# Layer norm's affine part as two fused operations on VectorE, sums of quarters reordered, last transposes among the first products, other banks in the recurrence

## The chip, the cores and the metric

The kernel runs on one core of one Trainium2 chip. A core has a matrix engine (TensorE, PE in the profile, with its weight loads as PEld), three engines for elementwise work (VectorE = DVE, ScalarE = ACT, GpSimd = POOL), and SyncE (SP), whose queue issues the transfers. SBUF is the memory on the core that the engines work on, PSUM its accumulators, of which this kernel uses eight banks of 128x512 fp32. The metric is device microseconds of one execution: the median of three runs. The profile is of one further execution, in which the hardware profiler records start and end of the instructions.

## The reference

One step of a trunk of two layers, over a prompt of 1024 tokens and 8 samples of 8 tokens (1088 tokens in all), width 1024, all in fp32. Each layer is a mixer (layer 0: RG-LRU, layer 1: HGRN2 with 8 heads) and a gated ffn with a causal convolution of width 3, both followed by a layer norm:

```python
def layer_norm(x, g, b):
    mu = jnp.mean(xf, axis=-1, keepdims=True)
    var = jnp.mean(jnp.square(xf - mu), axis=-1, keepdims=True)
    y = (xf - mu) * lax.rsqrt(var + LN_EPS) * g + b

def conv_ffn(x, buf, w_in, cw, cb, w_out):
    gate, up = jnp.split(x @ w_in, 2, axis=-1)          # 1024 -> 2 x 2816
    gc, new_buf = causal_dwconv(gate, buf, cw, cb)
    return (jax.nn.gelu(gc) * up) @ w_out, new_buf      # 2816 -> 1024

for i in range(DEPTH):                                  # trunk, DEPTH = 2
    mix = rglru_mixer(x, ...) if i % 2 == 0 else hgrn2_mixer(x, ...)
    x = layer_norm(ALPHA * x + mix, ln_g[i, 0], ln_b[i, 0])
    x = layer_norm(ALPHA * x + conv_ffn(x, ...), ln_g[i, 1], ln_b[i, 1])
```

The HGRN2 mixer projects x to q, f, v and g, forms decays from f, and per head and chunk of 64 tokens adds a masked product of q, k and the decays times v to what the carried state gives. Its output is normalised, gated by g and projected back. Besides the 1088 rows of output, the last states of both recurrences and of the convolutions are returned.

## The kernel before

**Precision.** Every fp32 matrix is split into a high part (rounded to the type fp32r) and a low part (the rest), and each product is three matmuls: high x high, high x low, low x high. So every weight and every activation must be split: one copy on ACT gives the high part, one subtraction on DVE or POOL the low part.

**Tiles and phases.** Tokens are tiled by 128: tiles m = 0 to 7 are the prompt, tile 8 holds the 64 sample tokens. z holds one row of 1024 fp32 per token; xa holds the transposed, split activations that feed the products. The phases are: mixer of layer 0 and its output projection (mix_out), ffn of layer 0 (phase 1), the HGRN2 mixer and its mix_out (phase 2), ffn of layer 1 (phase 3).

**The order of work is written by hand**: the instructions of each engine stand in the order in which the Python code calls them, and each engine runs its own in that order, waiting on semaphores for the others. `steps` is the list of steps, each with its weight blocks. A block's raw fp32 load is issued by SP (L140) into one of the buffers raw and rawf; `convert` splits it into a buffer of kind "b" (three, wb) or of kind "x" (wxf and wxb, there only inside an ffn, wx and wr elsewhere), with the high part on ACT (L214) and the low part on POOL or DVE (L215). A buffer comes free when its step ends. Work that may be squeezed between products waits in the queue `pend`: `fill()` runs one item, `flush()` all of them.

**The ffn's first product** is done on quarters, with 7 products of sums of quarters in place of 8 products. The activations' quarters b11, b21, b12, b22 come from the transposes of two tiles m and m + 4, four PSUM banks; `to_sums(m)` forms the seven sums and splits each (xc[0] to xc[6]): `put(c, src, eng)` is a high part on ACT (L392) and a low part on DVE or POOL (L393); L395 to L402 form the sums in scratch space of z. `to_sums(4)` does the samples. The weights' seven sums per block are formed by POOL (L176 to L182), split by ACT (L185) and POOL (L186). The first block of each ffn runs all seven products for the first 288 columns (the samples and the pairs 0 and 1), which accumulate in the four banks of psi, then for the other 256 (pairs 2 and 3), in the four banks of pss. `fills` gives the work to be called after product (i, c), i being the product and c the half.

**Layer norm** runs as a pipeline over tiles in `ln_pipeline`: `step_m` does the last projection of a tile and adds it to z (L413, with the row sums), `nrm_a` makes the row statistics on ACT (L424 to L426), `nrm_b` refines the reciprocal root on DVE (L431 to L434), normalises (L436, DVE) and multiplies by gamma (L438, on POOL, on DVE for the last two tiles of a mixer's norm), and `nrm_c` adds beta (L451, DVE) and stores the row (L456, to zsave or to the output). nrm_b runs one tile behind and nrm_c two; three behind comes `turn`, the transposes for the next phase. Behind a mixer the order of tiles is 8, 0, 4, 1, 5, 2, 6, 3, 7, so that to_sums(0) can begin after tile 4; the last two turns stand at i = 9 and in pend. The very last tile of the kernel is split between DVE (768 columns) and POOL (256).

**The ffn's second product** takes the 22 tiles of gelu(gate) * up in three groups. They are stored to ysave as they come and loaded again into xa; `y_part` splits them in two pieces, high on ACT (L1142), low on DVE (L1143). The last group takes four weight blocks and is the step inside the norm's pipeline.

**The recurrence** works by heads in periods: DVE and ACT make decays and scaled copies, PE grams (L1448), transposes (`kt_small`, L1533 and L1536), state products (`p_small`, with DVE's L1564 as evacuation), outputs (`o_small`), and the projections for the coming heads (`in_chunk`, L298 to L300, in psi banks) and for v (`v_step`, L1656 to L1658). `sbank` hands out a PSUM bank: of psi where run["bank"] is "in", else of pss.

Of the kernel before, what the change touches and what calls it, by code (L numbers as in the profile page):

```python
# [19 lines left out]
D = 1024  # L20
# [40 lines left out]
def hawk_hgrn2_convffn_deepnorm_kernel(  # L61
# [45 lines left out]
    run = {"dve": (), "ch": CH, "dma": 0, "cvt": 0, "phase": -1, "n": 0, "lo": dve}  # L107
# [86 lines left out]
    def convert():  # L194
# [166 lines left out]
    def to_sums(mp):  # L361
# [32 lines left out]

        act.copy(t1, b12)  # L395
        dve.tensor_tensor(t3, b22, t1, ALU.subtract)
# [31 lines left out]
    def nrm_b(m):  # L428
# [6 lines left out]
        for _, c in parts(m):  # L435
            dve.tensor_scalar(z[:r, m, c], z[:r, m, c], st[:, 2:3], st[:, 7:8], ALU.add, ALU.mult)  # L436
        for eng, c in parts(m):
            eng.tensor_tensor(z[:r, m, c], z[:r, m, c], gb[:r, 0, c], ALU.mult)  # L438

    def parts(m):  # L440

        if run.get("end") == m:
            return (pool, slice(768, D)), (dve, slice(0, 768))
        if m in run["dve"]:
            return (dve, slice(0, D)),
        return (pool, slice(0, D)),

    def nrm_c(m, final):
        r = rows_of(m)
        for eng, c in parts(m) if final == "out" and m >= NT - 3 else ((dve, slice(0, D)),):  # L450
            eng.tensor_tensor(z[:r, m, c], z[:r, m, c], gb[:r, 1, c], ALU.add)  # L451
# [10 lines left out]
    def ln_pipeline(step_m, junk, final=None, between={}, sums=False):  # L462
# [5 lines left out]
        run["dve"] = order[-2:] if sums else ()  # L468
# [7 lines left out]
        for i in range(NT + 2):  # L476
# [512 lines left out]
    def ffn(phase, li, final):  # L989
# [148 lines left out]
        def y_part(f, i):  # L1138

            y = yv[i]  # L1140
            for hi, lo in ((y[:, :SEQ], y[:, U + NS:]), (y[:, SEQ:U], y[:, U:U + NS])):
                act.copy(hi, lo.bitcast(F32))  # L1142
                dve.tensor_tensor(lo, lo.bitcast(F32), hi, ALU.subtract)  # L1143
# [40 lines left out]
        for p in range(NP):  # L1184
            f0, f1 = 2 * p, 2 * p + 1

            def gates(b, p=p, f0=f0, f1=f1):
# [3 lines left out]
                else:  # L1191
                    fills = {(5, 0): [flush]}
# [32 lines left out]
        for gi, grp in enumerate(GROUPS):  # L1225
# [27 lines left out]
            else:  # L1253
# [10 lines left out]
                stepf(phase, [out_blk(WO, f0, 0), out_blk(WO, f0, 1), out_blk(WO, f0 + 2, 0), out_blk(WO, f0 + 2, 1)], fn, "aaaa")  # L1264
# [260 lines left out]
    def kt_small(h):  # L1525
# [4 lines left out]
        for b0 in (0, 4):  # L1530
            ps = sbank("ps_kt")
# [295 lines left out]
```

## Time and profile before

| | us |
|---|---|
| median of 3 runs | 2615.56 (2613.95 to 2618.47) |
| the profiled execution | 2615.03 |
| its span, first to last instruction | 2613.3 |
| PE busy | 2506.9 (96%) |
| DVE busy | 1559.5 (60%) |
| POOL busy | 1378.8 (53%) |
| ACT busy | 951.9 (36%) |

The mean granted TensorE clock was 0.981 of full speed. A busy share is over the whole span; each phase has limits of its own. A row of waits names the waiting engine, the tile and line, what ended the wait, and the total, the number and the longest in us. A row of the timeline has the start and the duration in us, engine, line, operation, out<-in, shape and count; behind it, in brackets, the idle time ahead of it and what ended that. Lines such as L451 are those of the listing above. Records of a few matmuls are missing from the trace.

### The profile page before, as it was taken

The page shows a single profiled execution, that of the slowest core. Times are in us where ns is not written, and L with a number is a line of the kernel's source. Part 1 is how long each engine was busy: PE and PEld are TensorE (multiplying, and loading weights), DVE is VectorE, ACT ScalarE, POOL GpSimd, SP SyncE. Part 2 cuts the span into 40 slices and gives each one's busy share as a digit, 9 for nine tenths or more (in the row PEclk, how much of TensorE's full clock was granted, in tenths as well). Part 3 has the DMA queues.
Part 4 walks back from the last instruction along what each step waited for, and adds up shares of the span by engine and source line. Part 5 has one row for each costly group of instructions (what it writes and reads, how often), then busy time and mean ns, then how long its engine had stood idle before and what let it go on. Part 6 is the DMA issues. An engine that isn't in the chain of part 4 may idle for free. (4 is left out here: it accounts for less than half of the span.)

```text
span 2613.3 us, 39952 instructions
## 1 busy us (share of the span) xinstructions
PE 2506.9 (96%) x16007; PEld 2317.7 (89%) x16007; DVE 1559.5 (60%) x2431; ACT 951.9 (36%) x1643; POOL 1378.8 (53%) x1150
## 2 busy tenths in 40 slices
PE   9999969999999999999999999999799999999997
PEld 8999869999999788789898999977699999988886
DVE  4987376565656333658758485875656565562327
ACT  4775243333334011334444353453333333330113
POOL 2534378888876122235444452525788887842114
PEclk9999989999999999999999999999899999999999
DMA  4114022222224322122111111122222223264111
GB/s 131 41 45 165 32 81 66 84 66 91 74 85 169 134 100 83 49 83 58 48 34 42 50 42 42 50 88 99 73 84 67 83 67 95 77 227 136 58 41 72
DMA packets 205839, 209.79 MB, mean 80 GB/s; under 512 B 13201, under 2 KB 167953, under 8 KB 205614
## 3 DMA queue, kind: packets, MB, share of 16 engines
q1 hardware_dynamic: 205654, 207.25, 24.6%
q8 instruction: 126, 2.06, 0.3%
q14 instruction: 59, 0.48, 0.1%
HBM read 159.61 MB, written 47.61 MB: 79 GB/s over the span
## 5 line engine op out<-in xcount | busy, mean ns | idle before, releaser
L215 POOL TENSOR_TENSOR wb<-raw,wb 128x1024 fp32r<-128x1024 f32 (+1 forms) x77 | 201.2, 2616 | 618.4 <-ACT wb L214 415.7
L1057 PE MATMUL ps_f<-xa,wb 128*128 128x288 f32 (+1 forms) x3072 | 399.7, 290 | 15.0 <-ACT z L395 6.8
L1062 DVE TENSOR_TENSOR z<-z,ps_f 128x256 f32<-128x256 f32 (+2 forms) x550 | 196.0, 378 | 357.0 <-PE ps_f L1057 300.6
L1057 PEld LDWEIGHTS ps_f<-xa,wb 128*128 128x128 f32 x3072 | 392.5, 189 | 18.1 <-ACT z L395 7.6
L1057 PE MATMUL ps_f<-x,wb 128*128 128x288 f32 (+1 forms) x2496 | 323.0, 289 | 2.4 <-POOL wb L186 1.3
L1057 PEld LDWEIGHTS ps_f<-x,wb 128*128 128x128 f32 x2496 | 318.1, 189 | 3.2 <-POOL wb L186 1.7
L298 PE MATMUL ps_in<-xa,wb 128*128 128x384 f32 (+3 forms) x912 | 306.4, 336 | 5.7 <-ACT wb L214 5.5
L299 PE MATMUL ps_in<-xa,wb 128*128 128x384 f32 (+3 forms) x912 | 299.6, 329 | 0.3 <-DVE xa L356 0.3
L300 PE MATMUL ps_in<-xa,wb 128*128 128x384 f32 (+3 forms) x912 | 299.7, 329 | 0.0
L413 DVE SCALAR_TENSOR_TENSOR z<-z,ps_fo 128x512 f32<-128x512 f32 x128 | 87.8, 686 | 279.0 <-PE ps_fo L1162 266.5
L186 POOL TENSOR_TENSOR wb<-raw,wb 128x512 fp32r<-128x512 f32 x116 | 163.2, 1413 | 66.5 <-ACT wb L185 56.2
L186 POOL TENSOR_TENSOR wb<-rawf,wb 128x512 fp32r<-128x512 f32 x116 | 165.6, 1436 | 56.8 <-ACT wb L185 56.8
L214 ACT CAST wb<-raw 128x1024 fp32r<-128x1024 f32 (+1 forms) x83 | 82.0, 989 | 298.6 <-issue 183.1
L1110 DVE SCALAR_TENSOR_TENSOR z<-z,ptf 128x1104 f32<-128x1104 f32 x88 | 182.5, 2074 | 1.6
L298 PEld LDWEIGHTS ps_in<-xa,wb 128*128 128x128 f32 x912 | 172.9, 190 | 8.4 <-ACT wb L214 5.7
L299 PEld LDWEIGHTS ps_in<-xa,wb 128*128 128x128 f32 x912 | 173.1, 190 | 1.4 <-DVE xa L356 0.7
L300 PEld LDWEIGHTS ps_in<-xa,wb 128*128 128x128 f32 x912 | 172.4, 189 | 1.4 <-DVE wb L215 0.8
L1057 PE MATMUL ps_f<-xa,wxf 128*128 128x256 f32 (+1 forms) x1152 | 149.8, 288 | 2.7 <-ACT z L1077 2.7
L1057 PEld LDWEIGHTS ps_f<-xa,wxf 128*128 128x128 f32 x1152 | 146.6, 189 | 3.1 <-ACT z L1077 3.1
L185 ACT CAST wb<-rawf 128x512 fp32r<-128x512 f32 x116 | 71.1, 624 | 209.8 <-POOL rawf L182 76.0
L438 POOL TENSOR_TENSOR z<-z,gb 128x1024 f32<-128x1024 f32 (+2 forms) x32 | 88.6, 2767 | 103.4 <-DVE z L436 103.4
L185 ACT CAST wb<-raw 128x512 fp32r<-128x512 f32 x116 | 70.5, 625 | 182.9 <-POOL raw L182 63.6
(504 smaller groups left out, 5754.2 us busy)
## 6 DMA issues: line engine op xcount, KB each, us to landing
raw<-in_ffn_w_in_dram SPq DMA_DIRECT2D x44, 512.0 KB
rawf<-in_ffn_w_in_dram SPq DMA_DIRECT2D x44, 512.0 KB
ysave<-z SPq DMA_DIRECT2D x44, 512.0 KB
raw<-in_hg_w_in_dram SPq DMA_DIRECT2D x32, 512.0 KB
xa<-ysave SPq DMA_DIRECT2D x28, 544.0 KB
zsave<-z SPq DMA_DIRECT2D x24, 512.0 KB
raw<-in_ffn_w_out_dram SPq DMA_DIRECT2D x24, 512.0 KB
z<-zsave SPq DMA_DIRECT2D x24, 512.0 KB
```

Source lines behind the costliest of these rows:

```text
L185: act.copy(w[:, 0], src)
L186: run["lo"].tensor_tensor(w[:, 1], src, w[:, 0], ALU.subtract)
L214: act.copy(w[:, 0, :n], raw[:, :n])
L215: run["lo"].tensor_tensor(w[:, 1, :n], raw[:, :n], w[:, 0, :n], ALU.subtract)
L298: pe.matmul(ps[:, :n], lhsT=wh, rhs=xh, start=(k == 0), stop=False)
L299: pe.matmul(ps[:, :n], lhsT=wh, rhs=xl, start=False, stop=False)
L300: pe.matmul(ps[:, :n], lhsT=wl, rhs=xh, start=False, stop=(k == KT - 1))
L413: dve.scalar_tensor_tensor(zz, zz, a, ps, ALU.mult, ALU.add, accum_out=stat[:, m, n:n + 1] if acc else None)
L438: eng.tensor_tensor(z[:r, m, c], z[:r, m, c], gb[:r, 0, c], ALU.mult)
L1057: pe.matmul(ps[:, :n], lhsT=l, rhs=r, start=(kk == 0 and i < 4 and l is wh and r is xh), stop=(kk == 3 and l is wl), skip_group_check=(i > ...
L1062: dve.tensor_tensor(d, s, pv(ps), ALU.add)
L1110: dve.scalar_tensor_tensor(c[:, :L], gs[:, i:i + L], w[:, i:i + 1], c[:, :L], ALU.mult, ALU.add)
```

## The change

1. `nrm_b` keeps the statistics and does one scalar_tensor_tensor, (z - mean) * gamma; `nrm_c` does another, z * rstd + beta. Both are on DVE; POOL has no part in it, but for the split last tile of the kernel, which stays as it was.
2. `to_sums` issues the high parts of the quarters that come straight from PSUM first; DVE then has seven operations with none between them that waits for a high part made late. Two pieces of scratch in z change places.
3. The last two turns behind a mixer both go into pend. The first block's gate step calls `fill` after product 1 of the first half, and `flush` after product 5, so to_sums(2) and to_sums(3) stand among the products, both with pss banks. Before, to_sums(2) stood ahead of all products, with psi banks.
4. In `y_part` the low parts of odd tiles go to POOL.
5. The last group's four weight blocks are of a new kind "c": an x buffer if one is free, else a b buffer.
6. `kt_small` and `v_step` take psi banks.

The diff, its core:

```diff
@@ convert
+        if kind == "c":
+            kind = "x" if here and wfree["x"] else "b"
         if kind == "a":
...
-    def sbank(name):
-        if run.get("bank") == "in":
+    def sbank(name, tag=None):
+        if (tag or run.get("bank")) == "in":
             return psi.tile([P, 512], F32, name=name, tag="in")
         return pss.tile([P, 512], F32, name=name, tag="s")
...
@@ to_sums
-            s = [z[:, m, i * 512:(i + 1) * 512].rearrange("p (k t) -> p k t", t=n)
-                 for m in ((0, 4), (0, 4), (1, 8), (2, 6))[mp] for i in range(2)]
+            c0s = ((0, 512, 4096, 4608), (0, 512, 4096, 4608), (8192, 8704, 4096, TW), (2048, 2560, 6144, 6656))[mp]
+            s = [zf[:, c0:c0 + 512].rearrange("p (k t) -> p k t", t=n) for c0 in c0s]
...
+        hi(0, b11)
         act.copy(t1, b12)
+        hi(4, b21)
+        hi(6, b22)
+        lo(0, b11, dve)
         dve.tensor_tensor(t3, b22, t1, ALU.subtract)
+        hi(1, t3)
         dve.tensor_tensor(t1, t1, b11, ALU.subtract)
-        put(0, b11, dve)
+        lo(1, t3, pool)
         dve.tensor_tensor(t2, b22, t1, ALU.subtract)
-        put(1, t3, pool)
-        put(2, t2, pool)
+        hi(2, t2)
+        hi(3, t1)
+        lo(2, t2, pool)
         dve.tensor_tensor(t4, b21, t2, ALU.subtract)
-        put(3, t1, pool)
-        put(4, b21, dve)
-        put(5, t4, pool)
-        put(6, b22, dve)
+        hi(5, t4)
+        lo(3, t1, pool)
+        lo(4, b21, dve)
+        lo(5, t4, pool)
+        lo(6, b22, dve)
@@ nrm_b
-        for _, c in parts(m):
+        if run.get("end") != m:
+            dve.scalar_tensor_tensor(z[:r, m], z[:r, m], st[:, 2:3], gb[:r, 0], ALU.add, ALU.mult)
+            return
+
+        for _, c in END:
             dve.tensor_scalar(z[:r, m, c], z[:r, m, c], st[:, 2:3], st[:, 7:8], ALU.add, ALU.mult)
-        for eng, c in parts(m):
+        for eng, c in END:
             eng.tensor_tensor(z[:r, m, c], z[:r, m, c], gb[:r, 0, c], ALU.mult)
...
+    END = (pool, slice(768, D)), (dve, slice(0, 768))
@@ nrm_c
-        for eng, c in parts(m) if final == "out" and m >= NT - 3 else ((dve, slice(0, D)),):
-            eng.tensor_tensor(z[:r, m, c], z[:r, m, c], gb[:r, 1, c], ALU.add)
+        st = stat[:r, m]
+        for eng, c in END if run.get("end") == m else ((dve, slice(0, D)),):
+            if run.get("end") == m:
+                eng.tensor_tensor(z[:r, m, c], z[:r, m, c], gb[:r, 1, c], ALU.add)
+            else:
+                eng.scalar_tensor_tensor(z[:r, m], z[:r, m], st[:, 7:8], gb[:r, 1], ALU.mult, ALU.add)
@@ ln_pipeline
-            if final != "out" and 3 <= i < NT + sums:
+            if final != "out" and 3 <= i < NT:
                 turn(order[i - 3])
             run["bank"] = "s"
         if final != "out":
-            for m in order[NT - 1 if sums else NT - 3:]:
-                pend.append(lambda m=m: turn(m))
+            for m in order[NT - 3:]:
+                if not sums or m >= 4:
+                    pend.append(lambda m=m: turn(m))
@@ y_part
-                dve.tensor_tensor(lo, lo.bitcast(F32), hi, ALU.subtract)
+                (pool if i % 2 else dve).tensor_tensor(lo, lo.bitcast(F32), hi, ALU.subtract)
@@ gates
-                    fills = {(5, 0): [flush]}
+                    fills = {(1, 0): [fill], (5, 0): [flush]}
@@ the last group of the ffn's second product
-... fn, "aaaa")
+... fn, "cccc")
@@ kt_small
-            ps = sbank("ps_kt")
+            ps = sbank("ps_kt", "in")
...
-        ps = sbank("ps_kt8")
+        ps = sbank("ps_kt8", "in")
@@ v_step
-                banks = [sbank("ps_v")[:, :256] for _ in range(4)]
+                banks = [sbank("ps_v", "in")[:, :256] for _ in range(4)]
...
-                    ps = sbank("ps_v")
+                    ps = sbank("ps_v", "in")
```

Three places where instructions move. First PE at the turn from the HGRN2 mixer to its ffn; ps_o are the mixer's last projections, ps_t the transposes for to_sums, ps_f the ffn's products, wb and wxf weight buffers. Before:

```order
L620 MATMUL ps_o<-wb_86,xa 128x512
L373 MATMUL ps_t<-ident,z 128x128 x16
L1057 MATMUL ps_f<-xa,wb_84 128x288 x24
L1057 MATMUL ps_f<-xa,wb_85 128x288 x24
L1057 MATMUL ps_f<-x_2_15116,wb_86 128x288 x24
L373 MATMUL ps_t<-ident,z 128x128 x16
L1057 MATMUL ps_f<-x_2_15120,wxf_15591 128x288 x12
L1057 MATMUL ps_f<-xa,wb_84 128x256 x24
```

The same place after:

```order
L642 MATMUL ps_o<-wb_85,xa 128x512
L1079 MATMUL ps_f<-xa,wb_86 128x288 x24
L375 MATMUL ps_t<-ident,z 128x128 x16
L1079 MATMUL ps_f<-xa,wb_84 128x288 x24
L1079 MATMUL ps_f<-x_2_15098,wb_85 128x288 x24
L375 MATMUL ps_t<-ident,z 128x128 x16
L1079 MATMUL ps_f<-x_2_15102,wxf_15525 128x288 x12
L1079 MATMUL ps_f<-xa,wb_86 128x256 x24
```

The first 24 matmuls now stand ahead of the transposes of to_sums(2), and 48 between these and those of to_sums(3).

Second ACT at that turn; L185 are weight parts, L395 and L392 (L409 and L402 after) the activations' sums, L1069 and L1077 (L1091 and L1099) evacuations of products. Before:

```order
L426 ACTIVATE stat<-stat 128x1
L185 CAST wb_85<-raw_83 128x512
L185 CAST wb_85<-raw_82 128x512
L395 COPY z<-ps_t 128x512
L392 CAST xa<-ps_t 128x4x128
L392 CAST xa<-z 128x4x128 x3
L392 CAST x_2_15116<-ps_t 128x4x128
L392 CAST x_2_15116<-z 128x4x128
L392 CAST x_2_15120<-ps_t 128x4x128
L185 CAST wb_86<-raw_82 128x512
L185 CAST wb_86<-raw_83 128x512
L1069 COPY z<-ps_f 128x256
```

And after:

```order
L446 ACTIVATE stat<-stat 128x1
L185 CAST wb_84<-raw_83 128x512
L185 CAST wb_84<-raw_82 128x512
L185 CAST wb_85<-raw_82 128x512
L185 CAST wb_85<-raw_83 128x512
L1091 COPY z<-ps_f 128x256
L1091 COPY z<-ps_f 128x4x8
L185 CAST wxf_15525<-raw_82 128x512
L185 CAST wxf_15525<-rawf_15523 128x512
L402 CAST xa<-ps_t 128x4x128
L409 COPY z<-ps_t 128x512
L402 CAST x_2_15098<-ps_t 128x4x128
```

The casts of to_sums(2) stood between parts 3 and 4 of the first block's weights; now they stand behind all of them and behind the first part of the next block, cast from rawf, whose load SP issues behind the last tile's zsave.

Third ACT at the start of the last group of the first ffn (L1142, after L1164: y_part; L214, after L216: a weight block). Before, with the table load that begins the norm:

```order
L214 CAST wxf_2980<-rawf_2979 128x1024
L1142 CAST x_0_2500<-x_0_2500 128x1024
L1142 CAST x_0_2500<-x_0_2500 128x64
L214 CAST wb_84<-raw_82 128x1024
L214 CAST wb_85<-raw_83 128x1024
L465 ACT_TABLE_LOAD
```

and, at the end of the norm, where the HGRN2 weights come:

```order
L426 ACTIVATE stat<-stat 128x1
L355 CAST xa<-ps_t 128x4x128 x2
L214 CAST wb_86<-raw_82 128x1024
L214 CAST wb_84<-raw_83 128x1024
L214 CAST wb_85<-raw_82 128x1024
L1306 COPY ysh<-xa 128x1024
```

After, at the first place:

```order
L1164 CAST x_0_2500<-x_0_2500 128x1024
L1164 CAST x_0_2500<-x_0_2500 128x64
L216 CAST wxb_8009<-raw_82 128x1024
L216 CAST wb_84<-raw_83 128x1024
L487 ACT_TABLE_LOAD
L216 CAST wb_85<-raw_82 128x1024
L444 ACTIVATE junkf_8011,stat<-z,stat 64x1024
```

and at the second:

```order
L445 ACTIVATE stat<-stat,cst 128x1
L446 ACTIVATE stat<-stat 128x1
L357 CAST xa<-ps_t 128x4x128 x2
L216 CAST wb_86<-raw_83 128x1024
L216 CAST wb_84<-raw_82 128x1024
L1328 COPY ysh<-xa 128x1024
```

Block 2 of the group goes to wxb, and the first HGRN2 block (wb_85) is cast at the start of the norm; at its end there are two casts left instead of three.

More of the change, by code (lines that the diff above doesn't have):

```diff
@@ L106, in hawk_hgrn2_convffn_deepnorm_kernel @@
     steps = []
-    run = {"dve": (), "ch": CH, "dma": 0, "cvt": 0, "phase": -1, "n": 0, "lo": dve}
+    run = {"ch": CH, "dma": 0, "cvt": 0, "phase": -1, "n": 0, "lo": dve}
     blocks = []
@@ L393, in put, with hi_lo, hi, lo @@
             eng.tensor_tensor(lo, src, hi, ALU.subtract)
+        def hi_lo(c):
+            return (xc[c][:, :, h, t0:t0 + n] for h in range(2))
+        def hi(c, src):
+            act.copy(next(hi_lo(c)), src)
+        def lo(c, src, eng):
+            h, l = hi_lo(c)
+            eng.tensor_tensor(l, src, h, ALU.subtract)
+        hi(0, b11)
         act.copy(t1, b12)
+        hi(4, b21)
+        hi(6, b22)
+        lo(0, b11, dve)
         dve.tensor_tensor(t3, b22, t1, ALU.subtract)
+        hi(1, t3)
         dve.tensor_tensor(t1, t1, b11, ALU.subtract)
-        put(0, b11, dve)
+        lo(1, t3, pool)
         dve.tensor_tensor(t2, b22, t1, ALU.subtract)
-        put(1, t3, pool)
-        put(2, t2, pool)
+        hi(2, t2)
+        hi(3, t1)
+        lo(2, t2, pool)
         dve.tensor_tensor(t4, b21, t2, ALU.subtract)
-        put(3, t1, pool)
-        put(4, b21, dve)
-        put(5, t4, pool)
-        put(6, b22, dve)
+        hi(5, t4)
[3 more added lines that the diff above has]
+        lo(6, b22, dve)
     def resid(m, n, ps, scaled, acc=False):
@@ L434, in nrm_b @@
         dve.tensor_tensor(st[:, 7:8], st[:, 4:5], st[:, 6:7], ALU.mult)
-        for _, c in parts(m):
+        if run.get("end") != m:
+            dve.scalar_tensor_tensor(z[:r, m], z[:r, m], st[:, 2:3], gb[:r, 0], ALU.add, ALU.mult)
+            return
+        for _, c in END:
             dve.tensor_scalar(z[:r, m, c], z[:r, m, c], st[:, 2:3], st[:, 7:8], ALU.add, ALU.mult)
-        for eng, c in parts(m):
+        for eng, c in END:
             eng.tensor_tensor(z[:r, m, c], z[:r, m, c], gb[:r, 0, c], ALU.mult)
[L440 to L446, printed above, removed]
+    END = (pool, slice(768, D)), (dve, slice(0, 768))
     def nrm_c(m, final):
         r = rows_of(m)
-        for eng, c in parts(m) if final == "out" and m >= NT - 3 else ((dve, slice(0, D)),):
-            eng.tensor_tensor(z[:r, m, c], z[:r, m, c], gb[:r, 1, c], ALU.add)
+        st = stat[:r, m]
[4 more added lines that the diff above has]
+                eng.scalar_tensor_tensor(z[:r, m], z[:r, m], st[:, 7:8], gb[:r, 1], ALU.mult, ALU.add)
             if final == "out":
@@ L467, in ln_pipeline @@
         run["end"] = order[-1] if final == "out" else None
-        run["dve"] = order[-2:] if sums else ()
         def turn(m):
@@ L1262, in fn @@
                     ln_pipeline(sm, lambda: fs_["junk"], final, {1 + 2 * g: (lambda g=g: states(g)) for g in range(3)})
-                stepf(phase, [out_blk(WO, f0, 0), out_blk(WO, f0, 1), out_blk(WO, f0 + 2, 0), out_blk(WO, f0 + 2, 1)], fn, "aaaa")
+                stepf(phase, [out_blk(WO, f0, 0), out_blk(WO, f0, 1), out_blk(WO, f0 + 2, 0), out_blk(WO, f0 + 2, 1)], fn, "cccc")
         def close(_):
```

## The prediction

> **What bounds the kernel now.** I read the page first: busy shares and the 40 slices.
>
> ```profile
> PE 2506.9 (96%) x16007; PEld 2317.7 (89%) x16007; DVE 1559.5 (60%) x2431; ACT 951.9 (36%) x1643; POOL 1378.8 (53%) x1150
> PE   9999969999999999999999999999799999999997
> PEclk9999989999999999999999999999899999999999
> ```
>
> TensorE carries the span of 2613.3 us and is idle for 2613.3 - 2506.9 = 106.4 us of it. No product is removed, so what can be gained is idle time plus what matmuls lose at a lower granted clock. Slices 6 and 29 (both turns from a mixer to its ffn) show both at once, the last slice is the tail. Next the waits, to see what ends that idle time:
>
> ```profile
> PE ps_t L373 <- DVE z L451: 22.3, 4, 9.0
> PE ps_v L1656 <- DVE gb L1564: 7.3, 3, 2.4
> PE ps_f L1057 <- ACT z L395: 6.8, 2, 3.4
> PE ps_kt L1536 <- DVE A L1464: 5.7, 7, 1.4
> PE ps_in L298 <- ACT wb L214: 5.5, 1, 5.5
> PE ps_fo L1160 <- DVE z L413: 4.1, 2, 3.0
> PE ps_fo L1162 <- DVE xa L1143: 3.9, 2, 2.0
> ```
>
> The columns are total, number and longest wait in us. Each of these seven rows ends at a line that the diff touches or moves past; together they are 55.6 us. Third, windows behind such waits, since a wait costs more than itself:
>
> ```profile
> 1439.50:1445.40 5.90, 5.85 (x27) 5.85 (x28) 5.70 (x14) 1.99 (x2) 3.74 (x4) 0.50 0.01 3
> 1445.40:1448.90 3.50, 3.50 (x33) 3.50 (x32) 2.00 (x3) 0.00 (x0) 2.49 (x4) 1.00 0.71 200
> 1831.10:1848.10 17.00, 4.75 (x19) 4.36 (x20) 14.79 (x22) 5.74 (x12) 9.65 (x8) 0.50 0.08 32
> 851.50:854.90 3.40, 3.40 (x9) 2.64 (x8) 3.07 (x6) 0.09 (x1) 0.00 (x0) 0.50 0.26 105
> 1121.10:1128.00 6.90, 3.40 (x7) 2.30 (x8) 6.76 (x10) 4.29 (x8) 1.84 (x2) 0.51 0.30 101
> 2343.10:2349.90 6.80, 5.80 (x14) 4.54 (x15) 6.54 (x11) 0.00 (x0) 0.00 (x0) 0.50 0.97 366
> ```
>
> After the length come the busy times of PE, weight loads, DVE, ACT and POOL, then the granted clock. At 1439.5, behind a ps_v wait of 2.4 us, the clock is 0.50 for 5.9 us; then it is 1.00. Matmuls that ran 5.85 us at half clock need half of it at full clock, so that wait cost 2.4 + 2.9 us. The Trainium skill ("TensorE: Matmul & The Clock Gate", Part 1, The HAM clock gate) has the half rate come after an idle window of about 3.4 us. By it a wait of 2.4 us would cost only itself; the rows show half clock behind the shorter wait, and the measurement decides.
>
> **The parts and their costs.** The sum is made against the profiled execution, 2615.03 us; the median of the runs, 2615.56, is 0.5 above it, which is nothing beside the terms.
>
> *Normalisation in two fused operations.* Rows of min/median/max ns, then the window of the last norm stage:
>
> ```profile
> L436 DVE TENSOR_SCALAR z<-z,stat x37: 414/812/1728, 300.9 to 2605.9; 128x1024 f32<-128x1024 f32 x31, 64x1024 f32<-64x1024 f32 x4, 128x256 f32<-128x256 f32 x1, 128x768 f32<-128x768 f32 x1
> L438 POOL TENSOR_TENSOR z<-z,gb x32: 1026/2410/3447, 301.8 to 2606.1; 128x1024 f32<-128x1024 f32 x27, 64x1024 f32<-64x1024 f32 x4, 128x256 f32<-128x256 f32 x1
> L451 DVE TENSOR_TENSOR z<-z,gb x34: 1205/2230/3428, 309.4 to 2608.0; 128x1024 f32<-128x1024 f32 x30, 64x1024 f32<-64x1024 f32 x3, 128x768 f32<-128x768 f32 x1
> L1387 DVE SCALAR_TENSOR_TENSOR z<-z x6: 1273/1278/1293, 1162.9 to 1673.9; 128x1088 f32<-128x1088 f32 x6
> 2550.00:2599.00 49.00, 48.77 (x223) 39.09 (x222) 37.79 (x89) 16.59 (x38) 20.72 (x9) 1.00 0.18 61
> ```
>
> Before, DVE has L436 (0.81) and L451 (2.23 median, 1.21 at its fastest), POOL has L438 (2.41). After, DVE has two scalar_tensor_tensor, and POOL nothing. L1387 is that operation at 1088 columns: 1.28, so 1024 columns is about 1.2 us (estimate), the pair 2.4 against 0.81 + 2.23 = 3.04. In steady state this is worth nothing: PE is busy 48.77 of 49 us there. It counts at the tail, where nothing covers it:
>
> ```profile
> 2601.92 3.20 POOL L451 TENSOR_TENSOR z<-z,gb 128x1024 f32<-128x1024 f32 x1
> 2600.19 2.73 DVE L451 TENSOR_TENSOR z<-z,gb 128x1024 f32<-128x1024 f32 x1
> 2603.10 2.04 DVE L432 SCALAR_TENSOR_TENSOR stat<-stat 128x1 f32<-128x1 f32 x1
> L432 DVE SCALAR_TENSOR_TENSOR stat<-stat x36: 210/220/2035, 300.3 to 2603.1; 128x1 f32<-128x1 f32 x32, 64x1 f32<-64x1 f32 x4
> ```
>
> L432 works on one column, 0.22 us in its median, and took 2.04 here: it ends at 2605.14, POOL's operation at 2605.12. A DVE operation with two tensor inputs waits out a running POOL operation here. With POOL idle L432 loses about 1.8 us and L451, 2.73 against its fastest 1.21, about 1.5; nrm_c of tile 6 moves to DVE (+1.2), partly beside ACT's statistics of tile 7. **A: -2.0** (-1 to -2.5).
>
> *Transitions from mixer to ffn.* Now, at the second one:
>
> ```profile
> 1827.46 0.69 DVE L396 TENSOR_TENSOR z<-ps_t,z 128x512 f32<-128x512 f32 x1 [1.22 <-ACT z L395]
> 1834.12 0.68 DVE L413 SCALAR_TENSOR_TENSOR z<-z,ps_o 128x512 f32<-128x512 f32 x1
> 1845.13 2.30 DVE L451 TENSOR_TENSOR z<-z,gb 128x1024 f32<-128x1024 f32 x1
> 1845.31 3.12 PE L1057 MATMUL ps_f<-xa,wb 128*128 128x288 f32 x12 [3.39 <-ACT z L395]
> 1865.02 0.39 PE L1057 MATMUL ps_f<-xa,wb 128*128 128x256 f32 x1 [1.00 <-ACT xa L392]
> 1856.73 4.68 DMA rawf<-in_ffn_w_in_dram
> 1861.43 0.62 ACT L185 CAST wxf<-rawf 128x512 fp32r<-128x512 f32 x1 [0.51 <-DMA rawf<-in_ffn_w_in_dram]
> ```
>
> DVE's seven operations for one pair of tiles take 6.66 us (1827.46 to 1834.12) because it waits for ACT between them; reordered they run in 7 x 0.69 = 4.8. So the last residual (L413) starts at about 1831.7. Behind it, in DVE's order: statistics 0.9, fused b of tile 3, fused c of tile 6 (1835.7), statistics, b of 7, c of 3, c of 7, ending near 1840.9; now the load that is issued behind the last of them starts at 1856.73. The products no longer wait for tile 6: they follow the last projection at 1828 with 24 matmuls. But to_sums(2) now stands on ACT behind the whole of block 0's weights and part 0 of block 1, whose load SP issues behind tile 7's zsave: 1841 + 4.7 of transfer + 0.6 cast is about 1847. Then 4.9 us of to_sums(2) to 1852, the banks of to_sums(3) come free, its transposes and 12 products follow, and the second half of the columns starts at about 1855.3, not 1865.0: -9.7. If the three last fused operations take L451's 2.30 beside POOL's weight work, +3.0; half clock behind the new wait takes 2 (the window of 1831 lost 4.75 / 2 = 2.4). That leaves -4.7 to -9.7; I take -6, as POOL surely works there. The first transition has the same gaps (the waits count two of each). **B: -12** (0 to -24, the end if all of the two waits on L451 of 9.0, both on L395 and the clock went).
>
> *First hg weights in a freed wb.*
>
> ```profile
> 1123.45 2.00 ACT L214 CAST wb<-raw 128x1024 fp32r<-128x1024 f32 x2
> 1124.56 0.80 PE L298 MATMUL ps_in<-xa,wb 128*128 128x512 f32 x1 [5.46 <-ACT wb L214]
> 1063.86 0.50 PE L1166 MATMUL ps_fo<-wb,x 128*128 128x512 f32 x1 [0.41 <-POOL wb L215]
> ```
>
> The cast of block f goes before the norm stage, so 5.46 of waiting goes, and 3.40 / 2 = 1.7 of half clock (window 1121.1). Next late is block q, cast where f was; PE asks for it one chunk later, at 1119.1 + 24 x 0.21 = 1124.2 (24 matmuls of 512 columns, at twice the 3.50 / 33 us of those of 256 in the window of 1445.4), and it is there at about 1123.45 + 1.0 + 1.2 = 1125.7 (one of the two casts, and a low part on DVE). **C: -6** (-3 to -7.2). The price: in the last group block 2 takes wxb, read longer by the step before, so PE's wait at 1063.86 grows; between 0 and a whole POOL operation (2.4), nearer the present 0.41: +0.9 in each ffn. **F: +1.8** (0 to +5).
>
> *Banks in the recurrence.* ps_v and ps_kt no longer queue for a pss bank that DVE's L1564 or L1464 must release: 7.3 + 5.7 of waits and 3 x 2.9 of clock, 21.7 at most. But DVE's work there is untouched, and PE, once ahead, meets the next DVE or ACT result sooner, first at the gram products, where it already waits for DVE:
>
> ```profile
> PE ps_g L1448 <- DVE z L1428: 3.7, 3, 1.5
> ```
>
> I take half: **D: -10** (0 to -21.7).
>
> *Odd y_part on POOL.* At the turn to the ffn's second product:
>
> ```profile
> 2326.69 7.02 DVE L1143 TENSOR_TENSOR xa<-xa 128x1024 fp32r<-128x1024 f32 x4
> 2323.45 2.54 POOL L215 TENSOR_TENSOR wxf<-rawf,wxf 128x1024 fp32r<-128x1024 f32 x1 [8.59 <-ACT wxf L214]
> 2343.36 0.69 DVE L413 SCALAR_TENSOR_TENSOR z<-z,ps_fo 128x512 f32<-128x512 f32 x1 [6.29 <-DMA z<-zsave]
> ```
>
> Half of these subtractions go to POOL, at 2.4 each (L438), into 8.59 us in which it was idle, though later ones stand between its weight parts. DVE reaches the y products some 6 us sooner, and with them the stores and the reload of z that L413 waits for. At most the waits 3.9 + 4.1 and the clock 5.80 / 2 + 3.40 / 2 = 4.6 go: 12.6. POOL's queue takes some back. **E: -9** (-3 to -12.6).
>
> Sum: -2 - 12 - 6 + 1.8 - 10 - 9 = -37.2; 2615.03 - 37.2 = 2577.8.
>
> **Rivals.** (1) *DVE and the z reload take the waits back* in the recurrence and at the ffn's output: D and E are 0, leaving -18.2: **2597**. For it: the waits are short and many engines are close behind; against: L413's idle 6.29 is a DMA that is issued late, not slow.
>
> (2) *The new wait in the transitions*: the chain from c of tile 7 to part 0's load and to_sums(2) costs what the old wait did, B is 0: **2590**. For it: 1861.43 shows that very load ending a wait. Against: it starts 15 us sooner.
>
> (3) *Slower*: fused operations wait for POOL.
>
> ```profile
> L1110 DVE SCALAR_TENSOR_TENSOR z<-z,ptf x88: 1355/2156/3564, 399.0 to 2315.0; 128x1104 f32<-128x1104 f32 x88
> ```
>
> The same operation beside POOL takes 2.16, up to 3.56. In the last norm stage DVE is busy 37.79 / 49 = 77%, 4.5 us of a step of 5.8. With the pair at 2 x 2.07 in place of 3.04 a step is 5.6, the bound; each 0.1 us more adds 0.2 over 36 tiles, 7.2 us. At 2.6 us each the whole gain is gone; at 2.8, **2630**. Against: without L438 POOL has little left in these stages (it was busy 20.72 of 49 us with nine operations). The Trainium skill ("SBUF — State Buffer", SBUF: two separate sides) states that a GpSimd operation and a Vector operation with two tensor inputs hold their shared port pair alternately, each for its whole length. The ends of L432 and POOL's L451 at 2605.1 agree; the rule makes the fused pair blockable twice where L436 and L451 also were.
>
> (4) *The freed banks and places don't matter*: whatever PE gains, it waits for DVE elsewhere, and the time stays at **2615**.
>
> **Chances.** Forecast 0.60, (1) 0.18, (2) 0.12, (3) 0.05, (4) 0.05. The range 2558 to 2599 takes in (1) and (2) and on the low side B and D 20 us better; outside lie (3), (4) and a tenth. A change under 0.2% (5.2 us) can't be told from none: faster 0.90, same 0.05, slower 0.05.
>
> **What the profile after would show.** No L438 on POOL but one, the pair at 1.2 to 1.4 us each; ps_t waits of a microsecond or two instead of 9.0, and a new PE wait ahead of to_sums(3); no 5.46 at the hg start; no ps_v row among the waits; L413 waiting under 2 us for zsave. I am wrong if the pair runs above 2.1 us, if PE waits for rawf longer than 7 us, or if the gram products' waits grow by what ps_v lost.

## The result, and the profile after

The changed kernel took 2592.63 us (2588.93 to 2598.02, four runs), the kernel before, run beside it, 2614.76. The ratio is 0.9916 (0.9894 to 0.9938): 22 us faster. The forecast was 2578 (2558 to 2599). The profiled execution of the changed kernel is the slowest of its four, 2598.02 with a span of 2596.2; against the 2613.3 of before that is 17.1 us, and the following readings add up to these 17, not to the 22 of the medians. One execution of the last experiment below took 11338 us and is left out of its numbers. From the page, the busy times and PE's 40 slices:

```profile
PE 2506.6 (97%) x16007; PEld 2320.0 (89%) x16007; DVE 1538.2 (59%) x2384; ACT 951.2 (37%) x1643; POOL 1362.1 (52%) x1162
PE   9999979999999999999999999999799999999998
```

PE is as busy as before (2506.6, then 2506.9) in a shorter span: its idle time fell from 106.4 to 89.6 us. Slice 6 went from 6 to 7 tenths, the last from 7 to 8, but slice 29, the turn to the second ffn, still reads 7. PE's waits, longest totals first:

```profile
PE ps_f L1079 <- DVE z L1084: 18.3, 2, 10.1
PE ps_t L375 <- DVE z L473: 14.2, 4, 5.0
PE ps_in L300 <- ACT y8h L1371: 5.9, 5, 1.2
PE ps_fo L1182 <- DVE z L433: 3.0, 2, 2.0
PE ps_fo L1188 <- POOL wxb L217: 2.6, 2, 1.3
PE ps_fo L1184 <- POOL xa L1165: 2.2, 2, 1.1
```

The rows for ps_v, for ps_kt with L1464 and for the first hg product (5.5) are gone, and the 9.0 for tile 6 is 5.0. At the head stands a row that had no counterpart before: two waits of 8.2 and 10.1 us of the ffn's products for L1084, DVE's evacuation of an earlier product. To see what each part did, the same PE instruction is looked up in both traces; the shift between two such places is what the stretch won or lost (the first stretch begins with the span, and each holds more work than the part it is named after):

| PE instruction | before, us | after, us | shift | stretch since the row above |
|---|---|---|---|---|
| last product of ffn 1's first part | 839.65 | 841.74 | +2.1 | first turn (B) +2.1 |
| last of its second part | 1118.23 | 1120.98 | +2.75 | E and F +0.65 |
| first hg projection | 1124.56 | 1121.61 | -2.95 | C -5.7 |
| transposes of to_sums(0), layer 1 | 1805.93 | 1793.20 | -12.7 | recurrence (D) -9.8 |
| last product of ffn 2's first part | 2322.11 | 2312.40 | -9.7 | second turn (B) +3.0 |
| last of its second part | 2599.29 | 2584.81 | -14.5 | E and F -4.8 |
| end of the span | 2613.3 | 2596.2 | -17.1 | tail (A) -2.6 |

So A, C and D came about as large as foreseen, E at some two thirds, and the turns from mixer to ffn, which were to give 12 us, cost 5. The second turn, PE first, then ACT, DVE and SP:

```profile
1826.15 1.97 PE L375 MATMUL ps_t<-ident,z 128*128 128x128 f32 x8 [5.00 <-DVE z L473]
1847.03 3.25 PE L1079 MATMUL ps_f<-x,wb 128*128 128x288 f32 x12 [10.10 <-DVE z L1084]
1838.09 0.62 ACT L185 CAST wxf<-raw 128x512 fp32r<-128x512 f32 x1 [5.22 <-POOL raw L182]
1839.37 0.62 ACT L185 CAST wxf<-rawf 128x512 fp32r<-128x512 f32 x1 [0.66 <-DMA rawf<-in_ffn_w_in_dram]
1839.89 0.58 ACT L402 CAST xa<-ps_t 128x512 fp32r<-128x512 f32 x1
1840.50 0.69 DVE L406 TENSOR_TENSOR xa<-ps_t,xa 128x512 fp32r<-128x512 f32 x1 [6.39 <-ACT xa L402]
1846.01 1.50 DVE L1084 TENSOR_TENSOR z<-z,ps_f 128x256 f32<-128x256 f32 x6
1834.56 1.47 SPq L140 DMA_DIRECT2D rawf<-in_ffn_w_in_dram  x2
```

to_sums(2)'s transposes are done by 1828.1. Its first cast on ACT (L402) starts at 1839.89, behind the casts of part 6 (which waits 5.22 us for POOL's sum L182) and of the next block's part 0 (which waits for its load). DVE reaches to_sums(2) at 1834.1 and stands idle for 6.39 us; L1084, the evacuation of a product that had long been done, stands behind it in DVE's queue, and the product that wants that bank waits 10.1 us. Two clock windows of that stretch show what comes on top:

```profile
1838.00:1847.00 9.00, 0.00 (x0) 0.00 (x0) 5.55 (x12) 5.81 (x12) 5.97 (x6) 0.58 0.73 193
1846.90:1850.30 3.40, 3.27 (x14) 3.25 (x15) 0.60 (x3) 0.00 (x0) 1.77 (x2) 0.50 0.00 0
```

PE does nothing for nine microseconds and then runs 3.3 us at half clock; over the 3.1 us behind that the clock is 0.56. The fused operations by line (min, median and max in ns):

```profile
L456 DVE SCALAR_TENSOR_TENSOR z<-z,stat,gb x35: 1268/1278/2387, 301.2 to 2583.5; 128x1024 f32<-128x1024 f32 x31, 64x1024 f32<-64x1024 f32 x4
L473 DVE SCALAR_TENSOR_TENSOR z<-z,stat,gb x35: 1266/1276/2292, 308.1 to 2586.9; 128x1024 f32<-128x1024 f32 x31, 64x1024 f32<-64x1024 f32 x4
```

and the window of the last norm stage (length, busy PE, weight loads, DVE, ACT, POOL, clock):

```profile
2535.00:2584.00 49.00, 48.78 (x223) 39.34 (x224) 35.58 (x90) 16.54 (x38) 2.26 (x1) 1.00 0.18 64
```

Both have a median of 1.28 us; POOL's work in the last norm stage fell from 20.72 to 2.26 us in 49, and PE's share there is what it was, 48.78. The tail:

```profile
2585.70 2.47 DVE L473 SCALAR_TENSOR_TENSOR z<-z,stat,gb 128x1024 f32<-128x1024 f32 x2
2588.34 0.22 DVE L452 SCALAR_TENSOR_TENSOR stat<-stat 128x1 f32<-128x1 f32 x1
2591.41 1.36 DVE L471 TENSOR_TENSOR z<-z,gb 128x768 f32<-128x768 f32 x1
```

The column operation that took 2.04 beside POOL takes 0.22. And the stretch between the ffn's two parts, in the second ffn:

```profile
2318.07 2.64 DVE L1148 TENSOR_TENSOR z<-z 128x1024 f32<-128x1024 f32 x1
2320.63 2.42 DVE L1151 TENSOR_TENSOR z<-z 128x64 f32<-128x64 f32 x1
2322.98 1.36 DVE L1148 TENSOR_TENSOR z<-z 128x1024 f32<-128x1024 f32 x1
2324.26 2.42 DVE L1151 TENSOR_TENSOR z<-z 128x64 f32<-128x64 f32 x1
2323.22 3.37 POOL L217 TENSOR_TENSOR wb<-rawf,wb 128x1024 fp32r<-128x1024 f32 x1
2330.82 0.69 DVE L433 SCALAR_TENSOR_TENSOR z<-z,ps_fo 128x512 f32<-128x512 f32 x1 [4.14 <-DMA z<-zsave]
```

The four operations of the y products take 8.84 us. The second of 64 columns ends at 2326.68, POOL's L217 at 2326.59: DVE waits out POOL once more, here because POOL now has the odd low parts ahead of its weight parts. L433 still waits 4.14 us for its reload of z; the prediction had named under 2 us as the sign to look for.

### The profile page after: what moved, and what is told of

Its sections match the earlier page's. It is cut to its first block, busy times and chain, and to the rows that moved or that the text cites. A ratio compares the mean times of both kernels' runs of the same rounds, so it can differ in the third digit from the quotient of the medians.

```text
span 2596.2 us, 39881 instructions
## 1 busy us (share of the span) xinstructions
PE 2506.6 (97%) x16007; PEld 2320.0 (89%) x16007; DVE 1538.2 (59%) x2384; ACT 951.2 (37%) x1643; POOL 1362.1 (52%) x1162
## 5 line engine op out<-in xcount | busy, mean ns | idle before, releaser
L217 POOL TENSOR_TENSOR wb<-raw,wb 128x1024 fp32r<-128x1024 f32 (+1 forms) x76 | 199.1, 2622 | 523.1 <-ACT wb L216 293.4
L1084 DVE TENSOR_TENSOR z<-z,ps_f 128x256 f32<-128x256 f32 (+2 forms) x550 | 196.0, 378 | 358.5 <-PE ps_f L1079 301.8
L433 DVE SCALAR_TENSOR_TENSOR z<-z,ps_fo 128x512 f32<-128x512 f32 x128 | 87.5, 686 | 288.0 <-PE ps_fo L1184 278.2
L216 ACT CAST wb<-raw 128x1024 fp32r<-128x1024 f32 (+1 forms) x81 | 79.8, 986 | 233.2 <-issue 119.6
L185 ACT CAST wb<-rawf 128x512 fp32r<-128x512 f32 x116 | 71.0, 623 | 211.9 <-POOL rawf L182 76.0
L185 ACT CAST wb<-raw 128x512 fp32r<-128x512 f32 x116 | 70.1, 623 | 177.5 <-POOL raw L182 63.7
L1182 PE MATMUL ps_fo<-wb,xa 128*128 128x512 f32 x320 | 126.8, 396 | 3.0 <-DVE z L433 3.0
```

The lines of the kernel that those rows point to most:

```text
L185: act.copy(w[:, 0], src)
L216: act.copy(w[:, 0, :n], raw[:, :n])
L217: run["lo"].tensor_tensor(w[:, 1, :n], raw[:, :n], w[:, 0, :n], ALU.subtract)
L433: dve.scalar_tensor_tensor(zz, zz, a, ps, ALU.mult, ALU.add, accum_out=stat[:, m, n:n + 1] if acc else None)
L1084: dve.tensor_tensor(d, s, pv(ps), ALU.add)
L1182: pe.matmul(ps, lhsT=yh, rhs=wh, start=a, stop=False)
```

## The experiments

The theory (Q): the new wait comes from the places in three queues, ACT's (to_sums(2) behind the weight parts), DVE's (evacuations behind to_sums(2)) and PE's. Rivals: the fused operations are slow beside POOL and make DVE late (L); the load of the next block holds the chain (R).

**No weight parts ahead of to_sums(2).**

```diff
-                if first or c == 1:
+                if c == 1 or first and i > 1:
                     pump()
```

> The changed kernel, but in the first block no weight part is converted after the first two products of the first half, so to_sums(2) stands on ACT and DVE ahead of part 6 and of the next block's part 0. In the changed kernel the first evacuations on DVE (L1084) stand behind to_sums(2), which stands behind these parts, and PE waits 8.2 and 10.1 us for them. Theory Q (the place in the queues): both waits fall to 0 to 3 us, 14 to 17 us less in all, about 2576. Rival L (the fused operations, at 2.3 us beside POOL, make DVE late): the place of the parts changes little, 2588 to 2593.

Measured: 2579.38 us, ratio 0.9869 (0.9854 to 0.9885), 13 us less than the changed kernel, a little under the 14 to 17 expected. The second turn in its trace:

```profile
1816.11 1.97 PE L375 MATMUL ps_t<-ident,z 128*128 128x128 f32 x8 [5.00 <-DVE z L473]
1823.81 0.59 ACT L402 CAST xa<-ps_t 128x512 fp32r<-128x512 f32 x1
1830.96 1.85 PE L1079 MATMUL ps_f<-x,wb 128*128 128x288 f32 x12 [1.33 <-DVE z L1084]
```

From the transposes to the first cast are 7.7 us instead of 13.7, and the long wait is 1.33 instead of 10.10 (1.18 instead of 8.18 at the first turn). The fused operations stand as they were, so L is refuted as the cause of the wait. With the same transposes and the same norm, the place of a few casts decides 13 us.

**Only the next block's part goes behind.**

```diff
-                if first or c == 1:
+                if c == 1 or first and i != 1:
                     pump()
```

> The changed kernel, but only the next block's part 0, which needs the load that SP issues behind tile 7's zsave, goes behind to_sums(2); part 6 stays ahead of it. Theory Q: ACT reaches to_sums(2) when part 6's sum is ready on POOL, 1838.7 instead of 1839.9, so each long wait gets 1 to 1.5 us shorter, 2590. Rival R (the load is what holds the chain): the waits go as in the run before, about 2576.

Measured: 2589.78 us, ratio 0.9909 (0.9894 to 0.9923).

```profile
1832.09 0.62 ACT L185 CAST wxf<-raw 128x512 fp32r<-128x512 f32 x1 [4.24 <-POOL raw L182]
1832.62 0.58 ACT L402 CAST xa<-ps_t 128x512 fp32r<-128x512 f32 x1
1839.76 1.57 PE L1079 MATMUL ps_f<-x,wb 128*128 128x288 f32 x5 [6.30 <-DVE z L1084]
```

No load stands ahead of to_sums(2) any more, and waits of 7.0 and 6.3 remain, against 8.2 and 10.1 in the changed kernel and 1.2 and 1.3 with both parts behind. So the larger share, 5 to 6 us of each wait, was part 6, whose sum POOL makes late. R, as the only cause, is refuted; the load had some 1 to 4 us per turn.

**The transposes back ahead of the products**, with all else as changed.

```diff
-            if final != "out" and 3 <= i < NT:
+            if final != "out" and 3 <= i < NT + sums:
...
-            for m in order[NT - 3:]:
-                if not sums or m >= 4:
-                    pend.append(lambda m=m: turn(m))
+            for m in order[NT - 1 if sums else NT - 3:]:
+                pend.append(lambda m=m: turn(m))
...
-                    fills = {(1, 0): [fill], (5, 0): [flush]}
+                    fills = {(5, 0): [flush]}
```

> The changed kernel with the place of the last two turns undone: to_sums(2) ahead of all products again, with psi banks, to_sums(3) by the flush after product 5; the new norm, the reordered sums and all else stay. Theory Q: the move of the transposes lost what the shorter chain won, so without it each turn is some 5 us shorter than in the changed kernel, 2580 to 2586. If the move itself was worth something, it is slower than the changed kernel, 2597 to 2605.

Measured: 2582.69 us, ratio 0.9883 (0.9867 to 0.9898): 10 us faster than the changed kernel. So as it was made, the move of the transposes cost 10 us; with the parts placed right (the first run) it gains 3 over leaving them where they were (the four executions of each don't overlap, the intervals of the two ratios do). The two waits of the kernel before stand again, the one for tile 6 a little shorter (8.20 against 9.02). The one for the sums is 5.44, where before three waits of 3.39, 1.71 and 1.12 followed one another:

```profile
1817.71 1.97 PE L375 MATMUL ps_t<-ident,z 128*128 128x128 f32 x8 [8.20 <-DVE z L473]
1825.12 1.09 PE L1078 MATMUL ps_f<-xa,wb 128*128 128x288 f32 x3 [5.44 <-ACT z L409]
```

**The recurrence's banks back.**

```diff
-            ps = sbank("ps_kt", "in")
+            ps = sbank("ps_kt")
```

(and so for ps_kt8 and both of ps_v)

> The changed kernel with kt_small and v_step in pss banks again. Theory: the 12 us by which the recurrence got shorter come from the banks, so it is 10 to 14 slower, about 2604, and the three ps_v waits of 2.4 and the ps_kt waits stand again. Rival: they come from the freed POOL or from the other changes, and it stays at 2593.

Measured: 2602.76 us, ratio 0.9961 (0.9949 to 0.9974), 10 more than the changed kernel, and its waits again hold

```profile
PE ps_v L1678 <- DVE gb L1586: 7.3, 3, 2.4
PE ps_kt L1558 <- DVE A L1486: 4.6, 5, 1.4
```

So the 9.8 us of the table are the banks'. In the changed kernel PE's wait for ACT's L1371 (5.9 in five), the copy that takes a projection out of its bank, stands in their place, and it is not among the waits of this run: in_chunk's bank is now held by the evacuations of the projections themselves.

The next four runs stand on the first, since its turns no longer hide other parts. They ran on a second chip, on which the kernel before took 2612.93 against 2613.59 beside the first run.

**All low parts of y_part on DVE.**

```diff
-                (pool if i % 2 else dve).tensor_tensor(lo, lo.bitcast(F32), hi, ALU.subtract)
+                dve.tensor_tensor(lo, lo.bitcast(F32), hi, ALU.subtract)
```

> The kernel of the first run (to_sums(2) ahead of part 6, 2579.4), but all low parts of y_part on DVE again. Between the two products of the ffn's, the changed kernel won 5.7 us in the second ffn and nothing in the first, while DVE's y products (L1148 and L1151) grew from 2.9 to 8.9 us beside POOL. Theory P (POOL's share helps, and DVE's waits for POOL take half of it back): 5 to 7 slower, about 2585, and L1151 takes 0.22 us again. Rival: POOL's share brings nothing by itself, the gain came with the other parts; 2578 to 2581.

Measured: 2583.70 us, ratio 0.9887 (0.9873 to 0.9902), 4.3 more than the first run, a little under what was expected; the intervals of the two ratios overlap. In its trace the y products are short and late:

```profile
2306.70 1.23 DVE L1148 TENSOR_TENSOR z<-z 128x1024 f32<-128x1024 f32 x1
2307.84 0.22 DVE L1151 TENSOR_TENSOR z<-z 128x64 f32<-128x64 f32 x1
```

**Kind "a" for the last group.**

```diff
-                stepf(phase, [...], fn, "cccc")
+                stepf(phase, [...], fn, "aaaa")
```

> The kernel of the first run, but the last group's blocks of kind a again. Theory: the 5.5 us wait of the first hg product and its half clock come back (+5.7 to +7), and the two waits of 1.3 for wxb become 0.4 (-1.8): 2583 to 2585. Rival: the first hg block would be in time in any case now that POOL and DVE have less to do in the norm, and it is 1 to 2 faster, about 2578.

Measured: 2584.61 us, ratio 0.9890 (0.9875 to 0.9905), 5.2 more than the first run. The first hg product waits again, for 6.29 us:

```profile
1114.85 0.80 PE L300 MATMUL ps_in<-xa,wb 128*128 128x512 f32 x1 [6.29 <-ACT wb L216]
```

**The old norm.** The edit puts the old `nrm_b`, `parts` and `nrm_c` back into the first run's kernel.

```diff
-            dve.scalar_tensor_tensor(z[:r, m], z[:r, m], st[:, 2:3], gb[:r, 0], ALU.add, ALU.mult)
-            return
+        for _, c in parts(m):
+            dve.tensor_scalar(z[:r, m, c], z[:r, m, c], st[:, 2:3], st[:, 7:8], ALU.add, ALU.mult)
+        for eng, c in parts(m):
+            eng.tensor_tensor(z[:r, m, c], z[:r, m, c], gb[:r, 0, c], ALU.mult)
...
```

> The kernel of the first run with the old norm (tensor_scalar, gamma on POOL, beta on DVE). Theory: only the tail (+2.6) and the two turns, where tile 6 is waited for (+1 to +3 each), feel it: 2584 to 2588; inside the norm stages PE stays busy as before. Rival (the fused pair carries the gain in all four norm stages): more than 2590. Rival (it carries nothing): 2580 to 2582.

Measured: 2586.04 us, ratio 0.9892 (0.9875 to 0.9908), 6.7 more than the first run.

```profile
2574.09 2.04 DVE L452 SCALAR_TENSOR_TENSOR stat<-stat 128x1 f32<-128x1 f32 x1
1833.08 1.33 PE L1078 MATMUL ps_f<-x,wb 128*128 128x288 f32 x4 [4.94 <-DVE z L1083]
```

The tail has its 2.04 again, and from PE's last matmul to the end of the span are 13.9 us instead of 11.4. The rest is at the turns, where the wait for the evacuation is 4.94 instead of 1.33 and the one for tile 6 5.62 instead of 5.00. In the last norm stage PE stays busy with the old norm too (48.75 of 49 us); in the mixers' norms it waits once for the norm's result with each, 2.1 us with the new one and 1.4 and 1.9 with the old.

**Block 2 in a wb, block 3 in wxb.**

```diff
-                stepf(phase, [...], fn, "cccc")
+                stepf(phase, [...], fn, "cbbc")
```

> The kernel of the first run, with the last group's kinds c, b, b, c: block 2 goes to a wb that comes free some 0.9 us before wxb, block 3, needed later, to wxb. One wb stays free for the first hg block. Theory: the two waits of 1.3 for wxb fall to 0.4 or below, 1.8 less, about 2577.5; a version that beats both kernels. Rival: the wait moves to block 3, and nothing is gained, 2579.

Measured: 2575.95 us, ratio 0.9856 (0.9841 to 0.9870): 37 us faster than the kernel before. The waits for wxb fell from 1.3 to 0.2 in both ffns; that for the block now in wb is, in the first,

```profile
1055.29 0.50 PE L1188 MATMUL ps_fo<-wb,x 128*128 128x512 f32 x1 [0.38 <-POOL wb L217]
```

Two times 0.9 us come from that; the rest of the 3.4 to the first run, 1.6 us, is within the spread of runs.

The last four ran on this version, on a third chip.

**POOL's share of the low parts by place.**

```diff
-                (pool if i % 2 else dve).tensor_tensor(...)
+                (pool if i % 2 and i < 6 else dve).tensor_tensor(...)
```

> The version of the last run (to_sums(2) ahead of part 6, kinds c, b, b, c; 2575.95), with POOL's low parts in y_part only for the odd places below 6, which stand ahead of the y products; places 7, 9 and 11 on DVE. In the changed kernel the y products' small operations (L1151, 64 columns) took 2.43 us beside POOL's low parts and weight parts and 0.22 where POOL was idle. Theory P (DVE waits out POOL's operations there): POOL gets to its weight parts sooner, but DVE's y products meet these instead, 0 to 2 us better or the same, 2574 to 2576. Rival: the later places are where POOL's share pays, 2 to 4 slower.

Measured: 2577.28 us, ratio 0.9861 (0.9846 to 0.9876): the same.

```diff
+                (pool if i % 2 and i >= 6 else dve).tensor_tensor(...)
```

> The same version, POOL's low parts only for the odd places 7, 9 and 11, behind the y products; places 1, 3, 5 on DVE as in the kernel before. Theory: the wait of 1.9 us for place 5's low part comes back in each ffn, and the reload of z behind the y products is no earlier than in the kernel before; 3 to 5 slower, 2579 to 2581. Rival: the y products at 0.22 and 1.22 us again make up for it, 2575 to 2577.

Measured: 2596.53 us, ratio 0.9938 (0.9922 to 0.9955): 19 us slower than its neighbour, far beyond what was expected of it:

```profile
PE ps_fo L1182 <- DVE z L433: 9.1, 2, 4.9
PE ps_fo L1184 <- DVE xa L1165: 8.2, 2, 4.1
```

Those are its two longest waits at the ffn's second part (2.2 each in its neighbour's); in its timeline stand

```profile
2304.26 9.29 DVE L1165 TENSOR_TENSOR xa<-xa 128x1024 fp32r<-128x1024 f32 x4
2309.86 3.61 POOL L1165 TENSOR_TENSOR xa<-xa 128x1024 fp32r<-128x1024 f32 x2
2317.08 3.42 DVE L1148 TENSOR_TENSOR z<-z 128x1024 f32<-128x1024 f32 x1
2313.43 7.26 POOL L1165 TENSOR_TENSOR x<-x 128x1024 fp32r<-128x1024 f32 x4
```

DVE's last four operations on low parts, which stood beside POOL's weight parts before too (7.02), took 9.29 here, where POOL's first L1165 follows those, and the second y product, beside POOL's other four, 3.42 instead of 1.22. The two kernels differ only in the places, and the stretches from the end of an ffn's first part to the end of its second are 10.7 and 10.2 us longer here. So POOL's share is no gain in itself: three places on it ahead of the y products do as well as all six, and the same number behind them makes DVE late where PE waits for it. With all six on POOL those last three ran after the y products were done (POOL from 2306.06, the y products to 2303.8, in the trace of the version these runs stand on). The half clock adds to the waits (window 0.65):

```profile
2326.00:2334.00 8.00, 6.73 (x21) 5.35 (x22) 5.38 (x9) 0.00 (x0) 0.00 (x0) 0.65 0.96 375
```

**to_sums in the old order of operations**, by the lines of the diff above put back.

```diff
-        hi(0, b11)
         act.copy(t1, b12)
-        hi(4, b21)
-        hi(6, b22)
-        lo(0, b11, dve)
         dve.tensor_tensor(t3, b22, t1, ALU.subtract)
...
+        put(0, b11, dve)
```

> The same version with to_sums in its old order of operations. The trace of the changed kernel shows DVE's seven operations in 5.6 us for a pair of tiles, 6.7 before, where 4.8 was foreseen. Theory: some 1 us on the chain in each of the four waits of the two turns, 3 to 6 slower, about 2580. Rival: the order is covered by the weights' parts on POOL, 2575 to 2577.

Measured: 2579.37 us (2577.50 to 2582.29), ratio 0.9870 (0.9855 to 0.9885). The version itself ran on another chip only (2575.95); against the 2577.28 of the first of these four, which takes the same time, it is 2 us more, inside the spread of either: inconclusive. The waits for L1077, the line that is L1084 in the changed kernel, are longer in its trace, 7.5 in two against 3.9 in the version's:

```profile
PE ps_f L1072 <- DVE z L1077: 7.5, 2, 4.0
```

**Tile 6 first.**

```diff
             def mid():
+                if sums and i == NT - 1:
+                    nrm_c(order[i - 2], final)
                 if 0 <= i - 1 < NT:
                     nrm_b(order[i - 1])
...
-            if 0 <= i - 2 < NT:
+            if 0 <= i - 2 < NT and not (sums and i == NT - 1):
                 nrm_c(order[i - 2], final)
```

> The same version, but behind a mixer nrm_c of tile 6 stands ahead of nrm_b of tile 3 on DVE. PE waits 5.0 us at each turn for tile 6, and nrm_b of tile 3 takes 2.4 us ahead of it, a POOL operation being waited for. Theory: the wait falls to some 2 us and part of the half clock behind it goes, but weight part 2, now 1 us later on ACT, is what PE meets next; 2 to 5 faster, about 2572. Rival: the weights' parts take all of it back, 2575 to 2577.

Measured: 2578.43 us (median of three), ratio 0.9860 (0.9844 to 0.9877): no gain. The wait for tile 6 fell from 5.0 to 1.3, and PE then waits for weight part 2:

```profile
1805.80 1.09 PE L375 MATMUL ps_t<-ident,z 128*128 128x128 f32 x8 [1.26 <-DVE stat L451]
1811.86 0.85 PE L1081 MATMUL ps_f<-xa,wb 128*128 128x288 f32 x2 [4.96 <-ACT wb L185]
1809.49 1.15 ACT L444 ACTIVATE junk<-z,stat 128x1024 f32<-128x1024 f32 x1 [6.40 <-DVE stat L443]
```

POOL's sum for that part (L178) was done at 1808.1, some 3 us before ACT cast it at 1811.2; in between, the statistics of tile 7 (L444) stand ahead of it in ACT's queue and wait for DVE. What the one wait lost, the other took.

## Why the prediction was right or wrong

The time fell in the range and went the way that was forecast; the size was 22 us against 37. The range says little for the working: it had been drawn wide enough to take in rivals (1) and (2), and rival (2)'s 2590 came nearer to the 2592.6 than the forecast's 2578.

- **A, the tail**: -2.0 foreseen, -2.6 in the trace. The reason held to the row: L432's 2.04 became 0.22 with POOL silent, and came back with the old norm.
- **Steady state of the norm**: nothing foreseen, nothing there (48.77 and 48.78 us of 49). The fused operation was put at 1.2 us and takes 1.28.
- **B, the turns**: -12 foreseen, +5.1 found. This step failed. The working took PE's next wait to be the transposes of to_sums(3), for their banks, and let the 48 products between run on. It had seen that to_sums(2) stands behind the weight parts and the load on ACT, but gave DVE's queue only to_sums(2) and not L1084, which stands behind it there. Of the four products in that stretch PE ran three and then needed a bank that L1084 had to read first. The wait of 9.0 for tile 6 became 5.0, where a microsecond or two was the sign named, and a new wait of 8 to 10 us came on top, with half clock behind it. The first run shows that the new wait is the place of the weight parts alone; with it mended the turns give -5.4 and -4.1 (the same PE instructions looked up in its trace), close to what was foreseen. More than half of that isn't the move's: with the transposes left where they were (third run) the turns give -3.7 and -1.7, from the norm and the reordered sums. The rival that was told, a new wait that makes B zero, was the right one in kind, and was given 0.12; the load that it named was the smaller part of it, part 6 the larger (second run). The lower end of B's range doesn't follow from its rows either, as two waits of 9.0, both on L395 and the clock make 29.6, not 24; nothing hung on it.
- **C, hg start**: -6 foreseen, -5.7 found; without it the wait of 6.29 is back.
- **F, the price of it**: +1.8 foreseen; 0.41 became 1.29 in each ffn, +1.8. It was avoidable, by giving wxb to block 3.
- **D, the banks**: -10 foreseen as half of the bound; -9.8 in the table, -10 by undoing it. The half had been taken without a working, so the size is luck. What takes the rest is mainly not the gram products, as supposed, but a wait of 1.2 us for ACT's L1371 at the projections, in each of five places; the waits of the grams grew little (5.1 for L1450 against 3.7).
- **E, the second part of the ffn**: -9 foreseen; -5.9 found in the two stretches (-4.1 with F in them). The second mis-sized step: POOL's share was to bring DVE to the y products some 6 us sooner, and the stores and the reload of z with them. It did bring DVE there 6.7 us sooner in the second ffn (5.7 us behind the first part's last product, not 12.3), but the y products, 2.9 us when POOL is idle, take 8.84 beside it, so the last of them ends only 0.7 sooner. The reason stood in the prediction's own rows: DVE waits out POOL. In the first ffn almost nothing was left in the profiled execution (+0.65 with F); in the traces of the first four runs, which have the same code there, that stretch gives -1.8, so part of the shortfall is the spread of executions. But undoing POOL's share alone cost 4.3, half of the 9. With all low parts on DVE the two stretches are still 1.5 us shorter than before, F included, and what shortens them is not shown.

What was not weighed: that the sums' chain on DVE would still wait for ACT between its operations, once for 0.8 us or more. It was put at 4.8 us; for to_sums(2) it took 5.6, against 6.66 before, and for to_sums(3) 6.6 and 6.8.

## What to carry to other kernels

When work is moved in a program whose queues run in order, list for each engine what now stands behind the moved work, and look for evacuations (the operations that take a product out of its bank) among it: here the matrix engine, fed ahead of time, stopped at the first bank that nobody had emptied. A move should be tried with its feeders in two places, since the same transposes cost 10 us with the weight parts ahead of their casts and gained 3 with these behind. And work given to POOL was not free for DVE: count which DVE operations on the path run in those microseconds, and give POOL what is early and off the path.

## What the runs showed of the hardware

A DVE operation of 64 columns on SBUF operands took 0.22 us with POOL idle and 2.42 beside POOL, and the second of the two in the changed kernel ended within 0.1 us of POOL's operation. By the Trainium skill ("SBUF — State Buffer", SBUF: two separate sides) a Vector operation with two inputs in SBUF and a GpSimd operation that reads SBUF exclude each other for their whole length; these rows agree. What was new here is how far the place decides: the same share on POOL was worth 4 us ahead of the y products, and three places of it behind them cost 19 us against three ahead.

The half clock showed behind a wait of 10.1 us as the prediction's rows showed it behind one of 2.4: 0.50 for 3.4 us and 0.56 over the 3.1 after that, once PE had started again. Behind a wait of 4.9 it was 0.65 over 8 us.
